# A hybrid encoder trunk on one core: the MLP up-projection turned from feature-major to token-major

## The chip, the cores and the metric

The kernel runs on one core of one Trainium2 chip. The metric is the device time of one execution in microseconds (us). A core has a matrix engine (TensorE, PE in the profile, with its weight loads as PEld), a vector engine (VectorE, DVE), a scalar engine (ScalarE, ACT), GpSimd (POOL) and SyncE (SP), which here only issues loads. Each engine works through its own queue of instructions in order; semaphores tie the queues together. TensorE writes to PSUM, eight banks of 128 partitions by 512 float32; everything else lives in SBUF, 128 partitions wide.

## The reference, cut to what matters

Two layers act on 256 tokens of 2048 features. Each layer is a token mixer followed by a gated MLP with a width-3 convolution over the positions:

```python
def conv_ffn(h, w_up, conv_w, conv_b, w_down):     # h: [1, 256, 2048], w_up: [2048, 2*5632]
    u = h @ w_up
    u = lax.conv_general_dilated(u, conv_w[:, None, :], window_strides=(1,), padding=((1, 1),),
                                 dimension_numbers=('NWC', 'WIO', 'NWC'),
                                 feature_group_count=u.shape[-1]) + conv_b
    gate, val = jnp.split(u, 2, axis=-1)
    return (jax.nn.silu(gate) * val) @ w_down

for i in range(2):
    h = h + mixer(rms_norm(h, mix_norm[i]))         # grouped-query attention, then dilated windows
    h = h + conv_ffn(rms_norm(h, ffn_norm[i]), w_up[i], conv_w[i], conv_b[i], w_down[i])
return rms_norm(h, final_norm)
```

All is float32. The up-projection makes 11264 columns, 5632 of the gate and 5632 of the value: 22 blocks of 512 columns in each layer, which the kernel takes as 11 pairs of a gate block and a value block.

## The kernel before, in words

**Precision.** TensorE works on a rounded float32 format. To keep accuracy each operand is split into a rounded high part and a low part that holds the rest (xh and xl for activations, wh and wl for weights), and a product is three products: xh wh, xl wh and xh wl.

**Weights.** A weight tile, called a raw, is 128 partitions by 1024 elements, 512 KB. SyncE loads raws into six buffers. ScalarE rounds a raw to wh (line 119) and VectorE subtracts to get wl (line 120), in `split_raw`. The pairs of wh and wl stand in a ring of three (`NHL = 3`); a split can begin when TensorE has finished with the pair three tiles earlier. The program order puts a split `AHEAD = 45` instructions earlier than where it is written. During the down-projection a fourth pair (tag `wh9`, `wl9`, in the MLP's pool) joins the ring.

**Two ways to multiply.** The mixers' projections use `feed`, which is token-major: 128 tokens of activations are the stationary operand, 512 weight columns stream through, and the result has tokens on the partitions (lines 164 to 166; per raw 12 matmuls of 512 columns). The up-projection uses `feed_T`, which is feature-major: 128 weight columns are the stationary operand, and the activations stream, xh and xl side by side, 512 columns for wh (line 143) and 256 for wl (line 146). Per raw that is 8 matmuls of each. The result has features on the partitions and tokens along the free axis, which is what the convolution wants, since its taps are then one number per partition and its neighbours lie along the row.

**Order of the MLP.** `ffn` walks the pairs p in two halves of 6 and 5 (`HALVES`). For each pair and each half of 256 columns (hh) it feeds the gate, starts `up_post` for it, feeds the value and starts `up_post` for that. `up_post` is a generator; `step()`, called once per raw, advances the oldest pending one to its next yield, so that the work behind a block is spread among the matmuls of the next. In `up_post` ScalarE takes the xl half out of PSUM (446), VectorE adds the xh half (447) and multiplies by the tokens' rstd (449; the row of rstd was broadcast over partitions with a matmul by ones in `bcast_rstd`), ScalarE applies the centre tap and the bias (451), VectorE the two outer taps (456, 458), and ScalarE the silu for a gate (461). For a value GpSimd multiplies gate and value (466, or 474) and the result is split into high and low (289, 290). Tokens are kept in an even and an odd half, with a zero column between them, which is why taps read reversed halves.

**Seven products.** The down-projection `project_pair` takes some chunks of 512 features (`SKG`: the first and third pair of the first half, the first of the second) as seven block products in place of eight; `glu_forms` writes their operand sums. The other chunks are plain. `side` is a generator (`bias_lines`) that prepares mixer B's bias tables in spare steps of layer 0's MLP.

## Time and profile before

| | |
|---|---|
| median of three runs | 2300.83 us (2300.44 to 2301.5) |
| the profiled execution | 2300.93 us, span from first to last instruction 2299.2 us |
| TensorE busy | 2281.6 us, 99% |
| VectorE busy | 1732.5 us, 75% |
| ScalarE busy | 1248.6 us, 54% |
| GpSimd busy | 168.5 us, 7% |
| loads, share of the 16 DMA engines | 58.3% |
| granted TensorE clock | 0.999 |

How to read it: the profile takes one execution. A row of the groups names line, engine, operation, output and inputs, shapes and count; then busy time, mean duration in ns, and the idle time just before these instructions with what ended it. Overlapping instructions share busy time, so the spacing of matmuls is read from their starts. A row of a window has the stretch, its length, and for each engine the busy us with the number of instructions in brackets; the last three columns are the granted clock, the share of DMA and GB/s. A row of the chain or the timeline has the start, the duration, the engine and the line.

### The profile page before, as it was taken

What the parts mean: (1) busy time and instruction counts of PE and PEld (TensorE: products, weight loads), DVE (VectorE), ACT (ScalarE), POOL (GpSimd) and SP (SyncE); (2) the same over time, 40 slices, a digit from 0 to 9 for tenths busy, and PEclk for the clock granted to TensorE, in tenths of its full rate; (3) what the DMA queues carried; (4) which work ended last, traced back from release to release, by engine and by line L of the source; (5) the groups of instructions that cost most, each with busy time, mean ns of one, the idle gap of its engine ahead of it and who ended that gap; (6) DMA issues with size and microseconds to landing.
All of it is one profiled execution on the core that took longest, in us unless ns stands there. A gap on an engine that the chain in (4) does not pass through costs nothing.

```text
span 2299.2 us, 31196 instructions
## 1 busy us (share of the span) xinstructions
PE 2281.6 (99%) x11581; PEld 1935.0 (84%) x11581; DVE 1732.5 (75%) x2483; ACT 1248.6 (54%) x1802; POOL 168.5 (7%) x130
## 2 busy tenths in 40 slices
PE   9999999999999999999999999999999999999998
PEld 7788788888888888888888888878888888888886
DVE  6877887777877778878876876576777788777774
ACT  6565565555545556445454454445555555565553
POOL 2210000010001010010000000000101000001110
PEclk9999999999999999999999999999999999999999
DMA  8444565765666555666655555566565566565663
GB/s 300 154 141 156 189 197 175 245 202 186 207 196 191 186 184 181 207 215 202 190 176 178 178 188 168 176 190 192 189 192 187 173 217 202 184 191 185 202 211 128
DMA packets 260313, 437.54 MB, mean 190 GB/s; under 512 B 13904, under 2 KB 196944, under 8 KB 260160
## 3 DMA queue, kind: packets, MB, share of 16 engines
q1 hardware_dynamic: 258080, 429.84, 58.3%
q0 software_dynamic: 1648, 5.15, 0.8%
q8 instruction: 90, 1.47, 0.3%
q14 instruction: 63, 0.52, 0.1%
q10 hardware_dynamic: 432, 0.56, 0.1%
HBM read 429.20 MB, written 6.29 MB: 189 GB/s over the span
## 4 chain that ended last, share of the span: by engine, by line
PE 93%; DVE 3%; DMA 1%; issue 1%; POOL 1%; ACT 0%; SPq 0%; POOLq 0%; DVEq 0%; ACTq 0%
PE acc L143 28%; PE acc L146 14%; PE acc L165 11%; PE acc L166 11%; PE acc L164 11%; PE acc L272 5%; PE acc L274 5%; PE acc L277 5%; DVE wl L120 1%; DVE tT L333 1%; PE ps L304 1%; DMA raw<-in_w_up_dram 1%; PE ps L308 1%; PE ps L307 1%; PE ps L306 0%
## 5 line engine op out<-in xcount | busy, mean ns | idle before, releaser
L119 ACT ACTIVATE wh<-raw 128x1024 fp32r<-128x1024 f32 x822 | 866.4, 1059 | 780.0 <-PE acc L166 276.5
L120 DVE TENSOR_TENSOR wl<-raw,wh 128x1024 fp32r<-128x1024 f32 x822 | 1007.7, 1231 | 369.5 <-ACT wh L119 356.8
L143 PE MATMUL acc<-xh,wh 128*128 128x512 f32 x2816 | 707.2, 393 | 0.8 <-ACT wh L119 0.8
L143 PEld LDWEIGHTS acc<-xh,wh 128*128 128x128 f32 x2816 | 507.0, 189 | 93.2 <-ACT wh L119 1.6
L146 PEld LDWEIGHTS acc<-xh,wl 128*128 128x128 f32 x2816 | 384.1, 190 | 27.5
L146 PE MATMUL acc<-xh,wl 128*128 128x256 f32 x2816 | 392.6, 282 | 0.0
L165 PE MATMUL acc<-wl,xh 128*128 128x512 f32 x768 | 300.2, 391 | 3.5 <-DVE wl L120 2.1
L164 PE MATMUL acc<-wh,xh 128*128 128x512 f32 x768 | 301.8, 394 | 0.0
L166 PE MATMUL acc<-wh,xh 128*128 128x512 f32 x768 | 299.5, 390 | 0.0
L272 PE MATMUL acc<-wh,ah 128*128 128x512 f32 x524 | 205.7, 393 | 0.0
L274 PE MATMUL acc<-wh,al 128*128 128x512 f32 x524 | 205.2, 392 | 0.0
L165 PE MATMUL acc<-wl,ah 128*128 128x512 f32 x480 | 188.0, 392 | 2.0 <-DVE wl L120 1.8
L164 PE MATMUL acc<-wh,ah 128*128 128x512 f32 x480 | 187.8, 391 | 0.0
L166 PE MATMUL acc<-wh,al 128*128 128x512 f32 x480 | 187.3, 390 | 0.0
L165 PEld LDWEIGHTS acc<-wl,xh 128*128 128x128 f32 x768 | 144.4, 188 | 34.0 <-DVE wl L120 4.6
L166 PEld LDWEIGHTS acc<-wh,xh 128*128 128x128 f32 x768 | 144.2, 188 | 30.0
L164 PEld LDWEIGHTS acc<-wh,xh 128*128 128x128 f32 x768 | 144.4, 188 | 27.8
L277 PE MATMUL acc<-wl,ah 128*128 128x512 f32 x524 | 146.9, 391 | 0.0
L466 POOL TENSOR_TENSOR cv<-cg,cv 128x512 f32<-128x512 f32 x32 | 73.2, 2288 | 651.6 <-DVE cv L458 591.2
L272 PEld LDWEIGHTS acc<-wh,ah 128*128 128x128 f32 x524 | 98.4, 188 | 22.0 <-ACT wh L119 0.2
L277 PEld LDWEIGHTS acc<-wl,ah 128*128 128x128 f32 x524 | 98.4, 188 | 21.8
L274 PEld LDWEIGHTS acc<-wh,al 128*128 128x128 f32 x524 | 98.4, 188 | 21.6
(175 smaller groups left out, 1838.9 us busy)
## 6 DMA issues: line engine op xcount, KB each, us to landing
raw<-in_w_up_dram SPq DMA_DIRECT2D x352, 512.0 KB, 5.0
raw<-in_w_down_dram SPq DMA_DIRECT2D x176, 512.0 KB, 4.4
raw<-in_w_b_dram SPq DMA_DIRECT2D x144, 512.0 KB, 4.2
raw<-in_w_bo_dram SPq DMA_DIRECT2D x48, 512.0 KB, 3.7
raw<-in_w_a_dram SPq DMA_DIRECT2D x40, 512.0 KB, 3.7
raw<-in_w_ao_dram SPq DMA_DIRECT2D x32, 512.0 KB, 3.6
raw<-in_w_a_dram SPq DMA_DIRECT2D x16, 256.0 KB, 6.5
h<-in_x_dram SPq DMA_DIRECT2D x4, 512.0 KB
```

The source lines that it names most:

```text
L119: nc.scalar.activation(wh, r, AF.Copy)
L120: nc.vector.tensor_tensor(wl, r, wh.bitcast(F32), ALU.subtract)
L143: nc.tensor.matmul(acc[j], wh[:, kt, j * P:(j + 1) * P], lhs[4 * kg + kt][2], start=first and i == 0 and kt == 0, stop=False)
L146: nc.tensor.matmul(acc[j][:, :NT], wl[:, kt, j * P:(j + 1) * P], lhs[4 * kg + kt][0], start=False, stop=end and kt == 3)
L164: nc.tensor.matmul(accs[m], xh, wh[:, j, :], start=st, stop=False)
L165: nc.tensor.matmul(accs[m], xh, wl[:, j, :], start=False, stop=False)
L166: nc.tensor.matmul(accs[m], xl, wh[:, j, :], start=False, stop=sp)
L272: nc.tensor.matmul(acc[k], xh, wh[:, j, :], start=k in fresh, stop=False)
L274: nc.tensor.matmul(acc[k], xl, wh[:, j, :], start=False, stop=False)
L277: nc.tensor.matmul(acc[k], xh, wl[:, j, :], start=False, stop=last[k] == i and j == 1)
L304: nc.tensor.matmul(o, lh[ls], rh[rs], start=start, stop=stop)
L466: nc.gpsimd.tensor_tensor(cv, cg, cv, ALU.mult)
```

## The change

The up-projection goes through `feed`, token-major, like the mixers' projections. `feed_T` and `bcast_rstd` are gone. A block is now 512 columns at once, so a pair makes one gate block and one value block. The result has tokens on the partitions, and `up_post` turns it:

- ScalarE takes each of the two accumulators (128 tokens by 512 features) out of PSUM, scaled by the token's rstd, which is now one number per partition (line 420 of the changed kernel).
- VectorE transposes each 32x32 block in its place (421), for 128x512 at once.
- Sixteen copies of 32 partitions by 256 elements (4 groups of 128 features, 2 halves of tokens, 32 tokens) bring the 32x32 blocks to their partitions. A string, `PLACE`, gives each to an engine: nine to GpSimd (432), seven to ScalarE (434), none to VectorE.
- The taps, the silu and the product follow as before, in two halves (441, 445, 447, 450, 455 or 463).

Buffers: u has two of 1032 columns in place of three of 516; s and t, the scaled and the turned block, have one each; cg and cv have three each in place of two. The first pair of each layer uses `project2`, which does three quarters of K for gate and value first. A second pool `wp` is opened around the MLP's pool and takes the taps, six operand tags and the fourth buffer pair.

```diff
+PLACE = "pappaappapappapa"
...
-    def feed_T(acc, lhs, w, n, hh, kgs, first, last):
...
     def ffn(l, hT, ss_in, g_next, last, side=None):
-        with tc.tile_pool(name=nm("fpool"), bufs=1) as fp:
+        with tc.tile_pool(name=nm("wpool"), bufs=1) as wp, tc.tile_pool(name=nm("fpool"), bufs=1) as fp:
+            cw = wp.tile([P, 448], F32, name=nm("cw"))[:, :NROW]
...
-            us = [fp.tile([P, 528], F32, name=nm("u"))[:, :516].rearrange("p (j c) -> p j c", j=2) for _ in range(3)]
+            us = [fp.tile([P, 1040], F32, name=nm("u"))[:, :1032].rearrange("p (j c) -> p j c", j=4) for _ in range(2)]
...
-            def up_post(acc, n, hh, c, after=None):
+            def up_post(acc, n, cs, after=None):
                 u = us.pop(0)
                 us.append(u)
...
+                s = fp.tile([P, 2, 512], F32, tag="s", name=nm("s"))
+                t = fp.tile([P, 2, 512], F32, tag="t", name=nm("t"))
+                for m in range(2):
+                    nc.scalar.activation(s[:, m], acc[m], AF.Copy, scale=rstd[:, m:m + 1])
+                    nc.vector.transpose(t[:, m], s[:, m])
+                yield
+                tv = t.rearrange("p m (j q c) -> p j m q c", j=4, q=4)
+                uv = u.rearrange("p j (m t) -> p j m t", m=2)
+                for i in range(16):
+                    if i == 8:
+                        yield
+                    a, b = i // 4, (i // 4 + i) % 4
+                    dst = uv[32 * b:32 * b + 32, :, :, 32 * a:32 * a + 32]
+                    src = tv[32 * a:32 * a + 32, :, :, b]
+                    if PLACE[i] == "p":
+                        nc.gpsimd.tensor_copy(dst, src)
+                    elif PLACE[i] == "a":
+                        nc.scalar.activation(dst, src, AF.Copy)
+                    else:
+                        nc.vector.tensor_copy(dst, src)
+                for hh in range(2):
+                    yield
+                    c = cs[hh]
+                    for j in range(2):
+                        nc.scalar.activation(halves(c[:, j]), halves(u[:, 2 * hh + j])[:, :, :P], AF.Identity,
+                                             bias=tap(n, 2 * hh + j, 3), scale=tap(n, 2 * hh + j, 1))
...
+                    if p == 0:
+                        va = project2(w_up[l], p, NPAIR + p, hT, kgs, 1,
+                                      lambda a, cg=cg: start(up_post(a, 0, cg)))
+                    else:
+                        start(up_post(project(w_up[l], p, hT, kgs), p, cg))
+                        va = project(w_up[l], NPAIR + p, hT, kgs)
+                    start(up_post(va, NPAIR + p, cv, after))
...
-                hl_ring.insert(0, (fp, 9))
+                hl_ring.insert(0, (wp, 9))
```

What stands in a row on ScalarE while it finishes a value block of layer 0's first half (wh is the split of a coming tile, ah the high part of the gated product, v the copy out of PSUM, u and cv the convolution's input and output; in brackets, the queues whose semaphores it waits for). Before:

```order
L446 ACTIVATE v_4488<-acc_4234 128x256 [waits PE_49]
L446 ACTIVATE v_4488<-acc_4235 128x256 [waits PE_49]
L119 ACTIVATE wh_4549<-raw_4523 128x1024 [waits DMAHW6_49,DVE_49,PE_49]
L451 ACTIVATE cv_4231<-u_2603,cw_2602 128x256 [waits DVE_49]
L451 ACTIVATE cv_4231<-u_2603,cw_2602 128x256
L119 ACTIVATE wh_4573<-raw_4569 128x1024 [waits DMAHW3_49,PE_49,Activation_49]
L289 ACTIVATE ah_3994<-cv_4231 128x256 [waits Pool_49]
L289 ACTIVATE ah_3996<-cv_4231 128x256 [waits DVE_49]
```

And now, from the second evacuation on (s is the scaled block, t the turned one):

```order
L420 ACTIVATE s_4638<-acc_4416,rstd_2597 128x512
L120 ACTIVATE wh_4696<-raw_4669 128x1024 [waits DMAHW6_49,DVE_49,PE_49]
L434 ACTIVATE u_2607<-t_4639 32x8x32 [waits DVE_49]
L434 ACTIVATE u_2607<-t_4639 32x8x32 [waits Pool_49]
L434 ACTIVATE u_2607<-t_4639 32x8x32 [waits Activation_49] x2
L434 ACTIVATE u_2607<-t_4639 32x8x32 [waits Pool_49]
L434 ACTIVATE u_2607<-t_4639 32x8x32 [waits Activation_49]
L120 ACTIVATE wh_4723<-raw_4719 128x1024 [waits DMAHW7_49,PE_49]
L434 ACTIVATE u_2607<-t_4639 32x8x32 [waits Activation_49]
L441 ACTIVATE cv_4216<-u_2607,cw_2594 128x256 [waits Activation_49,Pool_49]
L441 ACTIVATE cv_4216<-u_2607,cw_2594 128x256
L441 ACTIVATE cv_4217<-u_2607,cw_2594 128x256
```

Seven placements and a tap that waits for GpSimd now stand between the splits, where two taps stood that waited for VectorE.

GpSimd's queue held one product for each half of a value block, and nothing between them. The first five of layer 0, before:

```order
L474 TENSOR_TENSOR cv_2628<-cg_2627,cv_2628 128x512 [waits DVE_49,Activation_49,Pool_49]
L474 TENSOR_TENSOR cv_2848<-cg_2847,cv_2848 128x512 [waits DVE_49,Activation_49]
L466 TENSOR_TENSOR cv_3075<-cg_3074,cv_3075 128x512 [waits DVE_49,Activation_49,Pool_49]
L466 TENSOR_TENSOR cv_3299<-cg_3298,cv_3299 128x512 [waits DVE_49,Activation_49,Pool_49]
L474 TENSOR_TENSOR cv_3525<-cg_3524,cv_3525 128x512 [waits DVE_49,Activation_49,Pool_49]
```

Now, for one value block, the two products behind its nine copies, and the next gate block's copies after them:

```order
L432 COPY u_2607<-t_4241 32x8x32 [waits DVE_49]
L432 COPY u_2607<-t_4241 32x8x32 x2
L432 COPY u_2607<-t_4241 32x8x32 [waits Pool_49] x4
L432 COPY u_2607<-t_4241 32x8x32 [waits Activation_49]
L432 COPY u_2607<-t_4241 32x8x32 [waits Pool_49]
L455 TENSOR_TENSOR cv_3804<-cg_3802,cv_3804 128x512 [waits DVE_49,Pool_49]
L455 TENSOR_TENSOR cv_3805<-cg_3803,cv_3805 128x512 [waits DVE_49]
L432 COPY u_2606<-t_4438 32x8x32 [waits DVE_49]
```

The first copy waits for VectorE's second turn of the block, several wait for an earlier copy into the same partitions, and one for a placement of ScalarE there.

112 lines of the change are left out of this document (29 added, 83 removed).

## The prediction

> **What bounds the kernel now.** I read the page first, for its busy shares and the chain that ended last, then the groups of instructions by line, then two windows and the chain in order of time. The page:
>
> ```profile
> span 2299.2 us, 31196 instructions
> ...
> PE   2281.6 (99%) x11581; PEld 1935.0 (84%) x11581; DVE 1732.5 (75%) x2483; ACT 1248.6 (54%) x1802; POOL 168.5 (7%) x130
> ...
> PE 93%; DVE 3%; DMA 1%; issue 1%; POOL 1%; ACT 0%; SPq 0%; POOLq 0%; DVEq 0%; ACTq 0%
> ```
>
> TensorE is busy for 99% of the span and carries 93% of the chain. So a change is worth what it does to the spacing of matmuls, less whatever it makes TensorE wait. The waits of the up-projection in the groups, with the prices that I need from them:
>
> ```profile
> L119 ACT ACTIVATE wh<-raw 128x1024 fp32r<-128x1024 f32 x822 | 866.4, 1059 | 780.0 <-PE acc L166 276.5 <-PE acc L143 209.9 <-PE acc L274 122.7
> L120 DVE TENSOR_TENSOR wl<-raw,wh 128x1024 fp32r<-128x1024 f32 x822 | 1007.7, 1231 | 369.5 <-ACT wh L119 356.8
> L143 PE MATMUL acc<-xh,wh 128*128 128x512 f32 x2816 | 707.2, 393 | 0.8 <-ACT wh L119 0.8
> L146 PE MATMUL acc<-xh,wl 128*128 128x256 f32 x2816 | 392.6, 282 | 0.0
> ```
>
> The matmuls of the up-projection waited 0.8 us in all. ScalarE's split L119 waited 209.9 us for TensorE to give a buffer pair back: the splits run ahead and are held by the ring of three pairs. The busy times of L143 and L146 overlap, so the spacing comes from the chain (one tile of weights, 512 KB, is 8 matmuls of L143 and 8 of L146), and for the token-major form, which the projections of the mixers use already, from a window of mixer B in which nothing else stands on TensorE:
>
> ```profile
> 673.18 1.84 PE acc L143 x8
> ...
> 843.57 1.84 PE acc L143 x8
> ```
> ```profile
> 1074.00:1109.00 35.00, 35.00 (x156) 1.00 0.68 211
> 700.00:880.00 180.00, 180.00 (x1035) 158.50 (x1034) 135.37 (x201) 105.63 (x158) 18.80 (x9) 1.00 0.60 188
> ```
>
> Between the two chain rows lie 61 tiles: 170.39 / 61 = 2.793 us each. The first window has about 155 starts of 512 columns in 35 us, or 0.2265; with the edges I take 0.227, and 12 of them, one tile token-major, are 2.725 us. In the second window, all up-projection, VectorE is busy for 75% and ScalarE for 59%.
>
> **The change part by part.**
>
> (1) Matmuls. The up-projection has 22 blocks of 512 columns in each of 2 layers, 8 tiles each: 352 tiles before and after. 352 x (2.793 - 2.725) = 23.9 us less, all on the path. Two matmuls of `ones` with the diagonal of rstd go too, under 1 us in all; I leave them out.
>
> (2) Work taken off and put on, per block of 512 columns, from these rows:
>
> ```profile
> L447 DVE TENSOR_TENSOR v<-acc,v 128x256 f32<-128x256 f32 x176 | 65.9, 416 | 0.0
> L449 DVE TENSOR_TENSOR u<-v,rbc 128x512 f32<-128x512 f32 x88 | 60.9, 692 | 2.8
> L446 ACT ACTIVATE v<-acc 128x256 f32<-128x256 f32 x176 | 56.4, 371 | 0.0
> L451 ACT ACTIVATE cv<-u,cw 128x256 f32<-128x256 f32 x88 | 48.2, 595 | 13.0 <-DVE u L449 13.0
> L458 DVE SCALAR_TENSOR_TENSOR cv<-u,cw,cv 128x256 f32<-128x256 f32 x88 | 38.5, 478 | 0.0
> L289 ACT ACTIVATE ah<-cv 128x256 fp32r<-128x256 f32 x84 | 30.7, 410 | 105.3 <-POOL cv L466 75.3 <-POOL cv L474 30.0
> L290 DVE TENSOR_TENSOR al<-cv,ah 128x256 fp32r<-128x256 f32 x84 | 32.6, 421 | 52.4 <-ACT ah L289 52.2
> L333 DVE STREAM_TRANSPOSE tT<-h 32x256 f32<-32x256 f32 x144 | 62.8, 436 | 2.6
> L677 ACT ACTIVATE stg<-acc,rstd 128x512 f32<-128x512 f32 x34 | 23.0, 680 | 9.8 <-PE acc L166 9.4
> ```
>
> VectorE loses 4 adds (L447) and 2 multiplications (L449): 3.05 us. It gains 2 turns of 128x512: L333 is 0.436 for 256 elements, and 256 more cost 0.27 (L449 against L447), so 0.70 each, 1.4 us. ScalarE loses 4 copies of L446 (1.5 us) and gains 2 scaled evacuations at 0.68 (L677) and 7 placements, priced as the plain copy L289, 0.41: 4.2 us. Against a tile time of 2.725 x 8 = 21.8 us per block: ScalarE 8 splits at 1.06 (8.5), 4.2, four L451 (2.4), half a silu and a share of L289 (1.4) make 16.5; VectorE 8 splits at 1.23 (9.8), 1.4, eight L456/L458 (3.8), L290 (0.8) make 15.9. Neither is full.
>
> (3) GpSimd gets 9 copies of 32 partitions x 256 elements per block. No such copy is in the trace. The rows on both sides of it:
>
> ```profile
> L797 POOL TENSOR_TENSOR t<-stg,st_q 128x256 f32<-128x256 f32 x16 | 17.1, 1100 | 80.7 <-ACT stg L677 80.7
> L729 POOL TENSOR_TENSOR ct_k<-rp,gb 128x128 f32<-128x128 f32 x2 | 0.9, 455 | 22.0 <-DMA gb<-in_k_gain_dram 22.0
> L49 POOL MEMSET ones<- 128x128 f32 x1 | 0.2, 205 | 0.0
> L431 POOL MEMSET u<- 128x2 f32 x6 | 0.4, 122 | 0.0
> ```
> ```profile
> 106.67 0.73 POOL L797 TENSOR_TENSOR t<-stg,st_q 128x256 f32<-128x256 f32 x1 [20.21 <-ACT stg L677]
> ```
>
> Above: a product with two inputs of the same 8 x 32 pattern, 0.73 undisturbed. Below: a fill that reads nothing; 128x2 to 128x128 adds 0.083, so 256 elements are 0.29. A copy reads one stream. The product adds 0.73 - 0.455 = 0.276 per 128 elements, 2.2 ns each, over a start of 0.18; half of that slope for one stream gives 0.18 + 0.28 = 0.46. I take 0.45 and keep 0.29 and 0.73 for the range.
>
> The mean of L797 is 1.10, not 0.73, and that matters more than the copy itself:
>
> ```profile
> 527.25 3.46 DVE L120 TENSOR_TENSOR wl<-raw,wh 128x1024 fp32r<-128x1024 f32 x2
> ```
> ```profile
> 527.39 2.24 POOL L466 TENSOR_TENSOR cv<-cg,cv 128x512 f32<-128x512 f32 x1 [20.11 <-DVE cv L458]
> ```
>
> The first subtraction ends at 527.25 + 1.23 = 528.48; GpSimd's product, issued at 527.39, ends at 529.63, 1.15 later; the second subtraction ends at 530.71, 1.08 after that. Each waited for the other to finish. The Trainium skill (SBUF — State Buffer, Who interferes with whom) says this as a rule: a VectorE instruction with two SBUF inputs and a GpSimd instruction that reads SBUF exclude each other for a whole instruction. By that rule, the trace agrees, with 1.15 and 1.08. So each copy is 0.3 us (0.45 less what runs before the lock) of VectorE's time where a subtraction is due, and one of the copies can sit behind a subtraction for 1.08.
>
> (4) The wait that is added. On ScalarE the convolution's centre tap (L441 after) needs all 16 placements, and behind it stand the next splits. How long may that last? A pair comes free when TensorE leaves it and is wanted two tiles on, 5.45 us later; the split takes 1.06 + 1.23. That leaves some 3 us.
>
> A value block, with 0 where TensorE ends it. ScalarE: the split of tile 2 to 1.25, the second evacuation to 1.85; VectorE: its subtraction to 2.5, the second turn to 3.15. GpSimd's nine copies from 3.15: 9 x 0.42 = 3.8, and behind the subtractions of tiles 3 and 4 twice 1.08, so 9.0. Three centre taps, 0.5 apart, then the split of tile 5 to 11.6. VectorE: five L445/L447 from 9.65, 0.4 apart as 0.478 with overlap, to 11.8; then the product of gate and value holds the lock for 1.15, to 13.0; the subtraction of tile 5 to 14.1. TensorE reaches tile 5 at 13.63 and needs its low half one matmul later, 13.85: it waits 0.25. For 22 value blocks, 5 us.
>
> A gate block has no product: four taps end at 11.2, the split of tile 5 at 12.2, the subtraction at 13.45. It makes it by 0.4. No loss, and nothing in hand.
>
> Three pairs in each layer write the seven operand sums: in the second half of such a block VectorE has eight operations of L290's kind where a plain one has two, 6 x 0.34 (0.42 with overlap) = 2.0 us, around the next block's first tiles, where the same count leaves a plain block about 1 us. I put 1 us on each: 6 us.
>
> (5) Free edits. The loads stay 352 of 512 KB, in longer runs; TensorE waited for none of them. If that cover went, a tile could come late by what the issue queue lost, which no row prices. The projection's last quarter of K in the first pair is needed 12 tiles in, 32.7 us, before 6 tiles in; it can only be less late. The fourth buffer pair is in another pool; only the down-projection uses it, and its matmuls wait as before. The u-gap fill is 2 instructions in place of 3.
>
> Sum: 2300.9 of the profiled execution (span 2299.2, the rest around it; the median of the runs is 2300.83, the same) - 23.9 + 5 + 6 = 2288.
>
> **The rivals.**
>
> A, the forecast: GpSimd's copy between 0.41 and 0.50. The loss per value block is 0 to 0.6, and the seven-sum blocks cost 3 to 6 us: 2280 to 2296. Chance 0.36.
>
> B, everything hidden: the copy at 0.40 or less. The last copy then starts before the subtraction of tile 4 asks for the lock, the taps begin at 3.15 + 9 x 0.38 + 1.08 = 7.7, and tile 5 is ready 0.65 early. Only the seven-sum blocks cost anything: 2277 to 2283. For it: a fill's 0.29. Against: no reading instruction on GpSimd is that fast here. Chance 0.25. The Trainium skill (GPSIMD Engine Reference, 4.1 Engine selection) says that one-input work on GpSimd runs at roughly line rate; by it the copy would be about 0.4 us, an estimate from that page's 1.2 GHz, and the sum 2280; no run here shows it.
>
> C, slower: GpSimd's chain of copies becomes what the taps wait for. At 0.73 the nine copies are 2.5 us longer; value blocks then lose 2.75 and gate blocks 2.1: 22 x 4.85 = 107, so 2300.9 - 23.9 + 107 = 2384. It decides from the copy price at which 44 blocks lose 24 us, 0.51. For it: the mean 1.10 of L797 beside VectorE's work. Against: half the input. Chance 0.19, for 2306 and above. The Trainium skill (Perfetto Trace Analysis, Optimizing Scalar/DVE Operations) warns that moving work between VectorE and GpSimd may not help because of the shared port; the rows above agree that there is a price, and C is where it wins.
>
> D, slower: ScalarE's placements cost what its patterned tap copy costs, 0.595 (L451), not 0.41: 7 x 0.19 = 1.3 us more ahead of the same split. Value blocks lose 1.0 more, gate blocks 0.8: 40 us, 2328. Against: L451 carries two per-partition operands, which the placement has not. Chance 0.10.
>
> E, no change: gain and waits cancel, copy at about 0.51: 2296 to 2306. Chance 0.10.
>
> **How the numbers follow.** Runs of this kernel spread by 1.1 us; 0.2%, 4.6 us, is about what can be told from no change. Faster is A and B, 0.61; same 0.10; slower C and D, 0.29. The likeliest is A, with its sum of 2288. The range goes from 2275, B with its full 24 us and a little, to 2330, which takes in D and the milder part of C and leaves out about 0.12 above. The faster cases alone are 2276 to 2296.
>
> **What would show it.** (1) Token-major chain rows 2.73 us per tile, and TensorE's busy share 98 to 99%. (2) GpSimd's copies: undisturbed 0.45, mean nearer 0.6. (3) In the releasers of the up-projection's matmuls, VectorE's low half (wl) with 5 to 15 us, most in value blocks at tile 5; if gate blocks wait as much, the copies are dearer than I took. (4) ScalarE's tap line waiting for GpSimd's copies, 1 to 2 us a block. (5) VectorE's subtraction with a mean of about 1.35. Wrong would be: GpSimd's copy over 0.5, a tap line waiting 4 us or more, or TensorE waiting for ScalarE's wh instead of wl.

## The result, and the profile after

The changed kernel takes 2330.5 us (four runs, 2327.7 to 2332.5) against 2300.9 beside it: a ratio of 1.0128, interval 1.0110 to 1.0145. It is slower, by 29.6 us, where 13 us faster were forecast. The page of the profiled execution, its busy shares and its chain:

```profile
span 2328.9 us, 28808 instructions
...
PE 2278.9 (98%) x10169; PEld 1859.0 (80%) x10169; DVE 1667.5 (72%) x2301; ACT 1366.7 (59%) x2022; POOL 388.4 (17%) x524
...
PE 72%; DVE 12%; POOL 7%; ACT 4%; issue 3%; DMA 3%; SPq 0%; DVEq 0%; POOLq 0%; ACTq 0%
```

TensorE has 1412 matmuls fewer, and its share of the chain fell from 93% to 72%: VectorE, GpSimd and ScalarE now stand on the chain for 23%. The groups that answer to those quoted before:

```profile
L121 DVE TENSOR_TENSOR wl<-raw,wh 128x1024 fp32r<-128x1024 f32 x822 | 1005.4, 1230 | 449.9 <-ACT wh L120 446.0
L432 POOL COPY u<-t 32x256 f32<-32x256 f32 x396 | 213.9, 540 | 827.7 <-DVE t L421 806.8
L434 ACT ACTIVATE u<-t 32x256 f32<-32x256 f32 x308 | 129.2, 420 | 52.3 <-POOL u L432 27.5 <-DVE t L421 18.4
L421 DVE STREAM_TRANSPOSE t<-s 128x512 f32<-128x512 f32 x88 | 62.1, 706 | 9.2 <-ACT s L420 9.2
L270 ACT ACTIVATE ah<-cv 128x256 fp32r<-128x256 f32 x84 | 30.7, 411 | 108.7 <-POOL cv L455 77.3 <-POOL cv L463 31.4
```

The prices are those of the forecast: the turn 0.706, the placement on ScalarE 0.420. GpSimd's copy has two durations: 338 of the 396 take under 0.45 us (median of all 0.40), the other 58 take 1.28 to 1.48, and the mean is 0.54. VectorE's subtraction keeps its mean, 1.230. What TensorE waited for (us in total, times, longest), after:

```profile
PE acc L146 <- DVE wl L121: 12.8, 20, 0.9
PE acc L258 <- DVE wl L121: 8.0, 11, 1.7
PE acc L253 <- ACT wh L120: 6.5, 7, 1.4
PE acc L145 <- ACT wh L120: 5.3, 3, 4.0
PE ps L393 <- DMA cr<-in_conv_dram: 2.0, 1, 2.0
```

L258 and L253 are the seven-product down-projection, whose matmuls waited for nothing before. The next table gives the eight MLP stages in us, read from the profiled execution, each from its first matmul to the first of the next stage (0a is layer 0's first half; `up` and `dn` are its projections; dn 0b and dn 1b are the seven-product part alone, up to the first plain matmul). Without a wait, token-major blocks need 21.8 us, so the up stages need 261.6 and 218.0. All that the table leaves out is within 0.4 us of each other in the first two rows; the last column is the median of the runs.

| kernel | up 0a | dn 0a | up 0b | dn 0b | up 1a | dn 1a | up 1b | dn 1b | median us |
|---|---|---|---|---|---|---|---|---|---|
| before | 274.5 | 126.6 | 223.4 | 53.6 | 269.8 | 126.9 | 223.5 | 53.7 | 2300.9 |
| changed | 285.4 | 132.6 | 221.6 | 58.2 | 272.3 | 132.1 | 221.8 | 57.8 | 2330.5 |
| GpSimd copies left out | 279.7 | 129.1 | 220.1 | 56.9 | 268.3 | 128.9 | 220.1 | 57.1 | 2309.0 |
| last blocks unplaced | 286.5 | 125.1 | 224.0 | 53.0 | 274.5 | 125.1 | 224.0 | 53.0 | 2313.7 |
| fourth pair in ring | 284.0 | 131.6 | 217.6 | 55.8 | 270.7 | 130.2 | 217.6 | 55.9 | 2315.1 |
| placements uncrossed | 284.6 | 129.4 | 222.4 | 57.0 | 272.1 | 128.6 | 222.6 | 58.2 | 2321.2 |
| product on VectorE | 280.0 | 127.7 | 217.9 | 55.4 | 266.2 | 127.4 | 217.8 | 56.6 | 2295.5 |
| same, idle product on GpSimd | 283.3 | 130.3 | 220.1 | 59.4 | 270.3 | 130.1 | 220.9 | 58.2 | 2319.5 |
| low half last | 281.8 | 133.0 | 218.4 | 59.4 | 268.5 | 132.1 | 218.4 | 59.7 | 2318.7 |
| best version | 268.2 | 125.1 | 217.6 | 53.0 | 262.5 | 125.1 | 217.6 | 53.0 | 2267.2 |

So the up-projections lost 9.8 us in sum and the down-projections 19.9, with nothing changed in the latter's own work. What happens at such a start, on ScalarE, GpSimd and TensorE in order of time (start, duration, engine, line; in brackets the idle time before and its releaser):

```profile
568.87 1.09 ACT L441 ACTIVATE cv<-u,cw 128x256 f32<-128x256 f32 x2 [1.56 <-POOL u L432]
569.87 1.04 ACT L120 ACTIVATE wh<-raw 128x1024 fp32r<-128x1024 f32 x1
...
582.56 0.72 ACT L270 ACTIVATE ah<-cv 128x256 fp32r<-128x256 f32 x2 [2.68 <-POOL cv L455]
583.19 1.04 ACT L120 ACTIVATE wh<-raw 128x1024 fp32r<-128x1024 f32 x1
```
```profile
561.15 7.69 POOL L432 COPY u<-t 32x256 f32<-32x256 f32 x9 [19.32 <-DVE t L421]
571.42 2.13 POOL L455 TENSOR_TENSOR cv<-cg,cv 128x512 f32<-128x512 f32 x1 [2.58 <-DVE cv L447]
579.18 3.35 POOL L455 TENSOR_TENSOR cv<-cg,cv 128x512 f32<-128x512 f32 x1 [5.63 <-DVE cv L447]
```
```profile
570.96 0.50 PE L253 MATMUL acc<-wh,ah 128*128 128x512 f32 x1 [0.54 <-ACT wh L120]
...
580.29 1.20 PE L258 MATMUL acc<-wl,ah 128*128 128x512 f32 x4 [0.88 <-DVE wl L121]
...
584.28 0.50 PE L253 MATMUL acc<-wh,ah 128*128 128x512 f32 x1 [1.41 <-ACT wh L120]
```

Twice ScalarE stands at an instruction that needs GpSimd: at the tap until the nine copies end (7.69 us in place of 9 x 0.40), and at ah until the product ends. The split of a coming tile (wh) is behind it in the queue, and TensorE waits for that split. I call this the queue-head theory. Its rivals: that GpSimd's work costs by holding up VectorE (port), or that the stretch simply holds too much work (supply).

### The profile page after: what moved, and what is told of

It reads as the page before. It is cut to its first block, busy times and chain, and to the rows that moved or that the text cites. A ratio compares the mean times of both kernels' runs of the same rounds, so it can differ in the third digit from the quotient of the medians.

```text
span 2328.9 us, 28808 instructions
## 1 busy us (share of the span) xinstructions
PE 2278.9 (98%) x10169; PEld 1859.0 (80%) x10169; DVE 1667.5 (72%) x2301; ACT 1366.7 (59%) x2022; POOL 388.4 (17%) x524
## 3 DMA queue, kind: packets, MB, share of 16 engines
q1 hardware_dynamic: 122912, 429.84, 56.6%
q8 instruction: 79, 1.29, 0.2%
## 4 chain that ended last, share of the span: by engine, by line
PE 72%; DVE 12%; POOL 7%; ACT 4%; issue 3%; DMA 3%; SPq 0%; DVEq 0%; POOLq 0%; ACTq 0%
PE acc L146 20%; PE acc L147 19%; PE acc L145 19%; DVE wl L121 5%; POOL u L432 4%; PE acc L258 4%; PE acc L253 3%; PE acc L255 3%; ACT wh L120 2%; POOL cv L455 2%; DVE tT L314 1%; DVE cv L445 1%; DVE cv L447 1%; POOL cv L463 1%; DMA raw<-in_w_up_dram 1%
## 5 line engine op out<-in xcount | busy, mean ns | idle before, releaser
L146 PE MATMUL acc<-wl,xh 128*128 128x512 f32 x2176 | 855.6, 393 | 13.5 <-DVE wl L121 11.1
L145 PE MATMUL acc<-wh,xh 128*128 128x512 f32 x2176 | 854.6, 393 | 5.9 <-ACT wh L120 5.3
L147 PE MATMUL acc<-wh,xh 128*128 128x512 f32 x2176 | 850.2, 391 | 0.0
L146 PEld LDWEIGHTS acc<-wl,xh 128*128 128x128 f32 x2176 | 409.8, 188 | 115.5 <-DVE wl L121 32.2
L145 PEld LDWEIGHTS acc<-wh,xh 128*128 128x128 f32 x2176 | 410.2, 189 | 93.0 <-ACT wh L120 8.4
L147 PEld LDWEIGHTS acc<-wh,xh 128*128 128x128 f32 x2176 | 409.7, 188 | 83.9
L432 POOL COPY u<-t 32x256 f32<-32x256 f32 x396 | 213.9, 540 | 827.7 <-DVE t L421 806.8
L253 PE MATMUL acc<-wh,ah 128*128 128x512 f32 x524 | 205.5, 392 | 6.7 <-ACT wh L120 6.5
L434 ACT ACTIVATE u<-t 32x256 f32<-32x256 f32 x308 | 129.2, 420 | 52.3 <-POOL u L432 27.5
L258 PE MATMUL acc<-wl,ah 128*128 128x512 f32 x524 | 148.4, 394 | 8.2 <-DVE wl L121 8.0
L258 PEld LDWEIGHTS acc<-wl,ah 128*128 128x128 f32 x524 | 96.7, 188 | 35.9 <-DVE wl L121 16.5
L253 PEld LDWEIGHTS acc<-wh,ah 128*128 128x128 f32 x524 | 98.3, 188 | 32.3 <-ACT wh L120 11.5
L255 PEld LDWEIGHTS acc<-wh,al 128*128 128x128 f32 x524 | 98.4, 188 | 20.3
L146 PEld LDWEIGHTS acc<-wl,ah 128*128 128x128 f32 x480 | 90.2, 188 | 23.9 <-DVE wl L121 5.7
L147 PEld LDWEIGHTS acc<-wh,al 128*128 128x128 f32 x480 | 90.1, 188 | 18.5
L145 PEld LDWEIGHTS acc<-wh,ah 128*128 128x128 f32 x480 | 90.2, 188 | 18.3
```

Source lines behind the costliest of these rows:

```text
L145: nc.tensor.matmul(accs[m], xh, wh[:, j, :], start=st, stop=False)
L146: nc.tensor.matmul(accs[m], xh, wl[:, j, :], start=False, stop=False)
L147: nc.tensor.matmul(accs[m], xl, wh[:, j, :], start=False, stop=sp)
L253: nc.tensor.matmul(acc[k], xh, wh[:, j, :], start=k in fresh, stop=False)
L255: nc.tensor.matmul(acc[k], xl, wh[:, j, :], start=False, stop=False)
L258: nc.tensor.matmul(acc[k], xh, wl[:, j, :], start=False, stop=last[k] == i and j == 1)
```

## The experiments

Ratios are to the kernel before, run beside each.

**The copies left out.**

```diff
-                nc.gpsimd.memset(u[:, :, P:P + 1], 0.0)
+                nc.gpsimd.memset(u, 0.0)
...
                     if PLACE[i] == "p":
-                        nc.gpsimd.tensor_copy(dst, src)
+                        continue
```

> The changed kernel with GpSimd's nine placement copies of every up-projection block left out (u is filled with zeros once instead, so nine sixteenths of each turned block never reach it and the values are not the reference's); ScalarE's seven placements, taps and products stay. Theory 'queue heads': splits come late because ScalarE and VectorE stand at instructions that wait for GpSimd, its copies and its products; without the copies the wait for them (1.56 us on ScalarE at 568.9 of the changed kernel's trace, followed by a TensorE gap of 0.9 us) is gone, the wait for the products stays: about 1.5 us in each of the four down-projection starts, 2 in each first pair and 0.1 in each plain value block, 2315 to 2322 us in all. Theory 'copies and port': the copies and what they do to VectorE are the loss, so about 25 us go, 2303 to 2308. Theory 'split supply': VectorE and ScalarE cannot deliver the short units' splits and sums fast enough whatever GpSimd does; down-projections stay at 132 and 58 us, 2326 to 2331.

2309.0 us, 1.0040 (1.0027 to 1.0054). Between the forecast of the queue heads (2315 to 2322) and that of copies and port (2303 to 2308): 21.5 us go, though the undisturbed copies are as cheap as 0.40. `Supply` falls.

**Splits placed earlier.**

```diff
-AHEAD = 45
+AHEAD = 70
```

> The changed kernel with AHEAD 70 in place of 45: the splits are placed further ahead of the side work in ScalarE's and VectorE's queues. Theory 'queue heads': some of the splits now stand before the instructions that wait for GpSimd; the down-projection starts lose 2 to 4 us less each and the first pairs 2 less: 2310 to 2322 us. Theories 'copies and port' and 'split supply': the same work in another order, within 4 us of 2330.

2324.9 us, 1.0104 (1.0089 to 1.0119): 5.6 us back, 2.6 and 2.1 of them in the long down-projections and at most 0.7 either way in any other stage. In the order of ScalarE, splits moved ahead of ah in the second half of the last block, not ahead of the taps. The time lies between the forecasts, 2.9 us above that of the queue heads and 1.1 below the others', so this run decides nothing.

**The fourth pair of buffers in the ring.**

```diff
                 slots, forms = {}, {}
+                if side is None and hf == 0:
+                    hl_ring.insert(0, (wp, 9))
...
-                hl_ring.remove((wp, 9))
+                if hf == 1:
+                    hl_ring.remove((wp, 9))
```

> The changed kernel with the fourth pair of split buffers in use in all of layer 1 and from the first down-projection of layer 0 on, where the changed kernel uses it in the down-projections alone. One more pair is 12 matmuls, 2.7 us, of work in hand. If the waits in the up-projection are bursts a little longer than the slack of three pairs, the up-projection stages that have the pair (3 of 4, which lose 3.6, 10.7 and 3.8 us against matmuls without a wait: 218.0, 261.6, 218.0) lose half of that or less, and the down-projection starts, whose ring is filled earlier, 2 us less each: 2312 to 2320 us. If VectorE and ScalarE lack time and not slack, the gain is under 4 us: 2326 to 2331. Layer 0's first up-projection half stays at 285 in both.

2315.1 us, 1.0058 (1.0043 to 1.0073), as the slack theory said. The second halves reach 217.6, no wait at all. Layer 1's first half gained only 1.6 and the stage ahead of it lost 4.3: the pair stood first in the ring and its first split came late there. I put that down to its buffer being shared with the stage before. This was not tried by itself; with the pair behind the others in the ring ("All of it together" below) the stage ahead loses nothing.

**The last value block of each half without turn and placements.**

```diff
-                    nc.vector.transpose(t[:, m], s[:, m])
+                    if n != short:
+                        nc.vector.transpose(t[:, m], s[:, m])
...
-                for i in range(16):
+                for i in range(0 if n == short else 16):
...
                 slots, forms = {}, {}
+                short = NPAIR + p1 - 1
```

> The changed kernel without VectorE's turn and without the sixteen placements in the last value block of each half (four blocks; their taps then read what the buffer held before, so the values are not the reference's). Theories 'queue heads' and 'copies and port': the down-projection starts lose their first part, the wait at 570 and before; 126 to 129 and 54 to 56 us in place of 132 and 58, 2314 to 2321 us in all; the wait for GpSimd's products (1.57 and 1.86 us) stays. Theory 'split supply': the turn's 1.4 us of VectorE alone are saved: at most 1.4 us in each of four, 2325 to 2330.

2313.7 us, 1.0056 (1.0039 to 1.0073). The down-projections fall to 125.1 and 53.0, below the kernel before and below the 126 to 129 and 54 to 56 forecast; `supply` (at most 1.4 us from each) falls here too. ScalarE still stands 98.3 us before ah in all, but TensorE has no wait at L253 or L258 any more. So the loss there comes from the turn and the placements of the last block, and the wait for the product alone does not make it. The up stages rose by 1.1 to 2.4, in their last two blocks; I take it that the shortened chain now meets the last tiles of the up-projection, which no run shows.

**Placements that do not cross.** Four placements write each row group of u; in the changed kernel both engines take turns at it, and each waits for the one before.

```diff
-PLACE = "pappaappapappapa"
+PLACE = "ppaapaapaappappa"
```

> The changed kernel with the placements shared out by the row group of u that they write: GpSimd has all eight that write rows 0 to 63, ScalarE all eight that write rows 64 to 127, so that none of the two engines' placements waits for one of the other's. In the changed kernel four placements of one row group are written in turn by both engines, each waiting for the one before. Theory 'crossed placements' (the 27.5 us for which ScalarE stood before its placements waiting for GpSimd's, with splits queued behind, are what leaving the copies out gave back): most of those 21.5 us come back without leaving anything out, 2311 to 2318 us. Theory 'copies and port' (the copies' own time and what they do to VectorE): one copy in nine fewer gives a ninth of it, 2326 to 2330.

2321.2 us, 1.0088 (1.0073 to 1.0103). Between the two forecasts. GpSimd has eight copies here in place of nine. ScalarE no longer waits at L434 for a copy (27.5 us before), though it waits 14.2 in place of 7.0 at the taps, and 9.4 us come back, 7.5 of them in the down-projections. That is less than half of what the copies cost. How the rest of their 21.5 us parts into their own time and their collisions with VectorE is not shown.

**The product's split one step later.**

```diff
                 nc.gpsimd.tensor_tensor(cv, cg, cv, ALU.mult)
                 yield
+                yield
```

The same line is added in `glu_forms`.

> The changed kernel with the splits of the gated product (ah, al) written one step later than the product on GpSimd, two steps of side work behind it and not one. Theory 'queue heads': ScalarE stood 77.3 and 31.4 us before ah, waiting for GpSimd's products, with splits behind it; one step later it stands less: each down-projection start loses 1.5 to 2 us less, each first pair 1 to 3 less, 2316 to 2323 us. If those waits were idle time that cost nothing: 2327 to 2333.

2325.5 us, 1.0106 (1.0091 to 1.0121). A miss: ScalarE's wait for the product grew (82.0 and 35.5 us for 77.3 and 31.4) and the first pairs kept their loss. The first up stage fell by 7.8, since the fetch gap of the next run did not occur there, and layer 0's first down-projection rose to 136.5. This rise is the same gap, moved by the extra step: SyncE issued eight stores at 539 to 550, and a fetch behind them came late. VectorE stood for it, and TensorE 5.3 us at 553.9:

```profile
539.24 3.07 SPq L888 DMA_DIRECT2D scr<-lnt  x4
544.55 5.07 SPq L888 DMA_DIRECT2D scr<-lnt  x4
```
```profile
551.45 1.23 DVE L222 TENSOR_TENSOR raw<-raw,raw 128x1024 f32<-128x1024 f32 x1 [6.92 <-DMA raw<-in_w_down_dram]
```

So only layer 1 shows what the edit does to a down-projection: 129.6 for 132.1 in its first half, 58.6 for 57.8 in its second.

**Two late transfers in layer 0.**

```diff
             def taps_gen():
-                yield
+                for _ in range(3):
+                    yield
...
-                    nc.sync.dma_start(dst[:, 32 * i:32 * i + 32, :], ln[:, :w])
+                    nc.gpsimd.dma_start(dst[:, 32 * i:32 * i + 32, :], ln[:, :w])
```

> The changed kernel with two edits in layer 0's first up-projection half, at places 150 us apart: the transposes of the taps come two steps later (TensorE waited 2.2 us for their rows at 278.7 and ran at half speed for a while behind it), and the stores of the bias lines go through GpSimd's queue, not through the one that fetches weights (a gap of 4.2 us at 433 behind eight stores that took 2.4 us each while fetches queued behind them). Theory 'late transfers': both gaps and the slow matmuls behind them go, the stage falls from 285.4 to 274 to 277 us and the whole to 2319 to 2322. If the fetches are late for another reason, the first gap alone goes: 281 to 282 and 2326 to 2327. Nothing else changes, the later stages within 0.5 us each.

2323.0 us, 1.0098 (1.0081 to 1.0115); the stage falls from 285.4 to 278.5, both about 1 us above the forecast. Both gaps are gone: the first block loses 1.5 in place of 5.1, and the block of the gap 0.4 in place of 7.4. Three later blocks lose 3.8 more together, beside the stores that GpSimd now issues. SyncE's queue held these stores beside the loads, eight of them from 406.8 to 423.8 with two fetches between them. With the stores on GpSimd's queue the gap occurs in none of the runs, and in the run of the later split, where eight fetches followed the first four stores, it did not occur at this place. The stores ahead of the weight fetches had thus made the 4 us gap.

**All of it together.** The last three edits, the fourth pair (behind the others in the ring), and ordinary units ahead of the first short one:

```diff
+                if hf == 0:
+                    first = "ccc" + "Pc" * 4 + "P" + "Pc" * 4 + "P" + "Pc" * 4 + "c"
+                else:
+                    first = "cccc" + "Pc" * 7 + "ccccc"
```

> The last three edits together, with the fourth pair of split buffers in the ring from layer 0's first down-projection on and in all of layer 1 (there behind the other three, since put first it waited for the stage before, 4.2 us), and with three or four ordinary units ahead of the first short product unit in the first down-projection pair of each half. If the losses are separate bursts, each with its own wait, the gains add up until nothing is left to lose: up-projections of 275 to 277, 218, 263 to 266 and 218 us, down-projections of 126 to 128 and 53 to 55, 2275 to 2290 us in all, faster than the kernel before. If they share one cause (VectorE and ScalarE too full), the sum stops near the best single edit: 2305 to 2312.

2303.8 us, 1.0012 (1.0003 to 1.0022). Between the two forecasts (2275 to 2290, and 2305 to 2312), close to the second. The up stages came as forecast (276.6, 217.6, 264.9, 217.6), the down-projections did not (134.5, 57.2, 129.1, 57.3). One wait had grown. ScalarE and GpSimd of this kernel at layer 1's start (ah is L270, the product L456):

```profile
1849.62 3.89 ACT L120 ACTIVATE wh<-raw 128x1024 fp32r<-128x1024 f32 x4
1860.69 0.42 ACT L270 ACTIVATE ah<-cv 128x256 fp32r<-128x256 f32 x1 [7.18 <-POOL cv L456]
```
```profile
1857.40 3.26 POOL L456 TENSOR_TENSOR cv<-cg,cv 128x512 f32<-128x512 f32 x1 [9.39 <-DVE cv L448]
```

The four splits ahead of ah use up the ring; then ScalarE stands 7.2 us, because the product began late, behind VectorE's taps and sums, and took 3.3 us.

**The product on VectorE.** This is the single edit with the largest gain; it is made in `glu` and in `glu_forms`.

```diff
-                nc.gpsimd.tensor_tensor(cv, cg, cv, ALU.mult)
+                nc.vector.tensor_tensor(cv, cg, cv, ALU.mult)
```

> The changed kernel with the gated products (44 of 128x512) on VectorE in place of GpSimd, nothing else. Theory 'queue heads': the product takes VectorE about 0.75 us (its 128x512 instructions with two inputs, estimated from the 0.42 us of the 128x256 ones) where GpSimd took 2.4 to 4.4 us and began after another engine's wait; ScalarE's wait before ah (77.3 and 31.4 us) shrinks to a third, and the down-projection starts lose 2 to 4 us less each, the first pairs 1 to 3 less: 2312 to 2322 us. Theory 'VectorE too full': 33 us more of work on the engine that is the tightest beside TensorE costs more than it gives: 2330 to 2340.

2295.5 us, 0.9978 (0.9969 to 0.9987): 35 us less than the changed kernel, 5 below the kernel before, and far below both forecasts (the lower was 2312 to 2322). The wait and the product in its groups:

```profile
L270 ACT ACTIVATE ah<-cv 128x256 fp32r<-128x256 f32 x84 | 31.0, 409 | 41.6 <-DVE cv L455 32.5 <-DVE cv L463 9.1
L455 DVE TENSOR_TENSOR cv<-cg,cv 128x512 f32<-128x512 f32 x32 | 21.9, 685 | 0.4
```

The product takes 0.685 us here and took 2.43 on GpSimd (L455 of the changed kernel); the wait before ah falls from 108.7 to 41.6 us. The ordinary value blocks, which lost 0.4 each, lose nothing, and the first pairs' largest loss falls from 5.0 to 2.3.

**The same edit in the kernel before,** as a control.

> A control: the kernel before, with its 44 gated products on VectorE in place of GpSimd and nothing else. In its trace ScalarE stood as long before ah, waiting for GpSimd's products (75.3 and 30.0 us), as in the changed kernel (77.3 and 31.4), yet TensorE has hardly a gap above 0.25 us in its up-projections and down-projection starts. If the wait costs only where the turned chain has used up the slack (theory 'queue heads' as an interaction), nothing is there to gain: 2297 to 2303 us. If the product on GpSimd costs as much in any kernel, the 35 us of the changed kernel would show here too: 2265 to 2280. If VectorE, with 33 us more of work, is too full in the kernel before: 2303 to 2315.

2300.3 us, 0.9999 (0.9989 to 1.0009): nothing to gain, as an interaction demands. The wait before ah in the kernel before, and in this one:

```profile
ACT ah L289 <- POOL cv L466: 75.3, 32, 3.1
```
```profile
L289 ACT ACTIVATE ah<-cv 128x256 fp32r<-128x256 f32 x84 | 30.6, 403 | 8.8 <-DVE cv L466 7.3 <-DVE cv L474 1.5
```

Some 96 of the 105 us of ScalarE's waiting went, and nothing was gained. So the wait costs only together with the change; the next figures show that the change used up much of what covered it.

**Where the cover went.** For each tile I took the time from the end of its low half's subtraction to its first matmul with that half. In us, median of a stage:

| kernel | up 0a | up 0b | up 1a | up 1b |
|---|---|---|---|---|
| before | 5.8 | 5.8 | 5.8 | 5.8 |
| before, low half first | 3.3 | 3.4 | 3.3 | 3.4 |
| changed | 2.1 | 2.2 | 1.8 | 1.8 |
| changed, low half last | 3.2 | 3.5 | 3.3 | 3.5 |
| product on VectorE | 2.6 | 3.0 | 2.4 | 2.8 |
| best version | 3.8 | 7.3 | 6.5 | 7.3 |

The changed kernel has a third of the cover, and 43 of its 352 tiles have less than 0.1 us; with the product on VectorE these are 10. Part of it is the order of matmuls in a unit. Feature-major, all eight with the high half came first; token-major, the second matmul wants the low half. Two runs change that order alone, one way in each kernel; in the first the edit is in `feed`, which the mixers use too:

```diff
                 nc.tensor.matmul(accs[m], xh, wh[:, j, :], start=st, stop=False)
-                nc.tensor.matmul(accs[m], xh, wl[:, j, :], start=False, stop=False)
-                nc.tensor.matmul(accs[m], xl, wh[:, j, :], start=False, stop=sp)
+                nc.tensor.matmul(accs[m], xl, wh[:, j, :], start=False, stop=False)
+            for m, kt in order:
+                (wh, wl), j = hls[kt // 2], kt % 2
+                xh, xl = at(lhs[4 * kg + kt], m)
+                nc.tensor.matmul(accs[m], xh, wl[:, j, :], start=False, stop=last and kt == 3)
```

> The changed kernel with the matmuls of a token-major unit in another order: first the four (or eight) pairs that use the high half wh, then those that use the low half wl; nothing else. wl is then used after 8 matmuls and not after 1, 1.6 us later. Theory 'order takes the slack': the 48 waits over 0.15 us between the first and the second matmul of a unit in the up-projections, 23.1 us in all and none over 1.6 us, are covered, less what comes back because VectorE is not let catch up: the up-projections lose 12 to 20 us less in all, the down-projection starts as before (they have this order already), 2308 to 2318 us. Theory 'total work in the way' (the queues are late whatever the order): the waits move to the next unit's wh, under 5 us gained, 2325 to 2331.

2318.7 us, 1.0078 (1.0063 to 1.0093). The up stages gain 14.0 us (3.6, 3.2, 3.8, 3.4), inside the 12 to 20 forecast; the down-projections lose 3.5 more. Outside the table, layer 0's first mixer takes 4.8 us less (264.7 for 269.5), which was not forecast, the next 0.8 less and the end 2.4 more. The whole is just above its range, and would be further above without the mixer. In the kernel before:

```diff
             for kt, j in order:
                 nc.tensor.matmul(acc[j], wh[:, kt, j * P:(j + 1) * P], lhs[4 * kg + kt][2],
                                  start=first and i == 0 and kt == 0, stop=False)
-            for kt, j in sorted(order, key=lambda o: o[1]) if end else order:
                 nc.tensor.matmul(acc[j][:, :NT], wl[:, kt, j * P:(j + 1) * P], lhs[4 * kg + kt][0],
                                  start=False, stop=end and kt == 3)
```

> The kernel before with the feature-major units in the opposite order: each matmul with the low half right behind the one with the high half, where all eight with the high half stood first. If the order alone made the difference, 10 us or more are lost, 2310 to 2325. If the order takes 1.6 us of a slack of 5.8 us and the rest is the longer chain of the turned blocks, hardly a wait appears: 2300 to 2304 us.

2305.6 us, 1.0022 (1.0012 to 1.0032), 1.6 above the upper range. The cover falls to 3.4 us and still TensorE waits 0.8 us for the low half in all its up-projection; the 5 us come without waits, as 2.7 us in each second half. The order is worth 2.4 us of cover in this kernel and 1.1 to 1.7 in the changed one, out of about 4 that went. I put the rest down to the turned block's chain; no run parts it.

**Port or queue head?** GpSimd repeats the product into a scratch tile that nobody reads, behind VectorE's own.

```diff
+                nc.vector.tensor_tensor(cv, cg, cv, ALU.mult)
-                nc.gpsimd.tensor_tensor(cv, cg, cv, ALU.mult)
+                nc.gpsimd.tensor_tensor(junk().rearrange("p (j t) -> p j t", j=2), cg, cv, ALU.mult)
```

> The kernel with the products on VectorE (2295.5 us), and beside it GpSimd multiplies the same 44 pairs of 128x512 again into a scratch tile that nobody reads, right behind VectorE's product. GpSimd works and reads as much as in the changed kernel, and its next placement copies still stand behind the product, but nobody waits for the product. Theory 'queue heads': ScalarE's wait for the product was the cost; 2295 to 2302 us. Theory 'port': GpSimd's product beside VectorE's two-input instructions was the cost; 2322 to 2332.

2319.5 us, 1.0077 (1.0060 to 1.0094): neither forecast. 24 of the 35 us that moving the product had gained are lost again. The ordinary value blocks stay at no loss, as queue heads said. The first pairs lose as much as in the changed kernel (5.4 and 4.4 in the first halves, 2.3 in the second) and the down-projections nearly as much (378.0 us in all for 380.7, and 367.1 without the idle product), although nobody waits for this product. VectorE's small instructions beside it, in this kernel, in the changed one, and in the one with the product on VectorE, from which this run differs by the idle product alone:

```profile
L271 DVE TENSOR_TENSOR al<-cv,ah 128x256 fp32r<-128x256 f32 x84 | 45.5, 573 | 0.0
L445 DVE SCALAR_TENSOR_TENSOR cv<-u,cw,cv 128x256 f32<-128x256 f32 x88 | 57.0, 666 | 5.6 <-ACT cv L441 5.6
```
```profile
L271 DVE TENSOR_TENSOR al<-cv,ah 128x256 fp32r<-128x256 f32 x84 | 32.6, 421 | 54.1 <-ACT ah L270 54.0
L445 DVE SCALAR_TENSOR_TENSOR cv<-u,cw,cv 128x256 f32<-128x256 f32 x88 | 44.9, 524 | 5.7 <-ACT cv L441 5.6
```
```profile
L271 DVE TENSOR_TENSOR al<-cv,ah 128x256 fp32r<-128x256 f32 x84 | 32.3, 417 | 0.0
L445 DVE SCALAR_TENSOR_TENSOR cv<-u,cw,cv 128x256 f32<-128x256 f32 x88 | 40.1, 475 | 3.8 <-ACT cv L441 3.7
```

The idle product starts a little later than the real one and falls on al and the next taps: these take 0.15 us longer in the mean than in the changed kernel, 25 us over both rows, and 0.16 and 0.19 longer than without the idle product. So GpSimd's product costs VectorE time though nobody waits for it. The next copies stand behind it in GpSimd's queue as well, and ScalarE's wait for them at L434 rises from 21.9 to 28.6 us. How the loss in the changed kernel's first pairs and down-projection starts parts between port and queue head is not settled, since the idle product collides with other instructions than the real one did.

**A version that beats both.** The edits of "All of it together", with the product on VectorE in place of the later step:

> The kernel of the last run of all edits together, with the products on VectorE in place of one step later. There one wait was left in each down-projection start: ScalarE stood 7.2 us at ah for a product that GpSimd began late and took 3.3 to 4.4 us for, with the next splits behind it, and TensorE waited 2.1 to 3.4 us and then ran slowly for 3.4 us. Theory 'queue heads': that wait falls below what four pairs of buffers cover, the down-projections come to 126 to 128 and 53 to 55 us, and the whole to 2284 to 2292 us, faster than the kernel before. Theory 'VectorE too full': 2300 to 2310.

2271.5 us, 0.9872 (0.9857 to 0.9887), below the forecast. The same without the reordered units:

> The same without the ordinary units put ahead of the short ones in the down-projections. If the short product units at the start, with their sums and splits on VectorE beside the last value block's chain, take part in the loss, the four down-projection starts lose 1 to 3 us more each: 4 to 10 us above the run with them. If the wait for GpSimd alone made it, within 2 us of that run.

2275.2 us, 0.9889 (0.9872 to 0.9905): 3.8 us of loss, 3.1 of it in the down-projections and just under the 4 to 10 forecast, so the short units at the start take a small part. And with the low half last:

> The best version so far (2271.5 us) with the same order of matmuls in its token-major units. Its up-projections of layer 0's first half lose 6.6 us against 261.6 and layer 1's 0.9; 'order takes the slack' gives 3 to 6 us: 2265 to 2269. 'Total work in the way': 2270 to 2273.

2267.2 us, 0.9855 (0.9840 to 0.9869), 33.7 us less than before. The time is in the forecast range, but not for its reason: all eight stages are as in the 2271.5 us version, to 0.1 us, and the 4.3 us come from layer 0's first mixer, 4.7 us shorter, which uses the same `feed`. The engines' shares of its chain, and what TensorE still waited for in these projections:

```profile
PE 86%; DVE 0%; issue 0%; ACT 0%; POOL 0%; POOLq 0%; DVEq 0%
```
```profile
PE acc L145 <- ACT wh L120: 0.9, 2, 0.7
PE acc L150 <- DVE wl L121: 0.6, 1, 0.6
```

Three of its four up stages lose under 1 us and all four down-projections none; the 6.6 us left are in layer 0's first half. The up stages take 965.9 us in all, 25.3 less than before: where little waits, the token-major form is worth what step (1) said. Of the rest, 4.6 us are in the down-projections and 3.5 in the mixers and at the end. The edits that a feature-major kernel can have too (the fourth pair, the late transfers, the order of units) were not tried on the kernel before, so the 33.7 us are not the form's alone.

## Why the prediction was wrong

The sum against the trace: before, the up stages took 991.2 us in all; 352 tiles at 2.725 are 959.2. The changed kernel's took 1001.0, a loss of 41.8, and the down-projections 19.9 more than before: 2300.9 - 32.0 + 41.8 + 19.9 = 2330.6.

(1) Matmuls: right, 21.8 us per block wherever nothing waits. The gain was 32.0, not 23.9, since the stages before were 8.1 us longer than 352 tiles at 2.793.

(2) Work on VectorE and ScalarE: right in each price (0.706, 0.420, 0.676 for the scaled evacuation). "Neither is full" held in the mean and decided nothing.

(3) GpSimd's copy: 0.40 undisturbed, below the 0.45 taken. That is rival B's condition, for which 2277 to 2283 was forecast, so the copy's price was not what decided. The collision was read rightly (58 copies of 1.28 to 1.48 us), but it did not lengthen the subtractions: mean 1.230, where 1.35 was to show.

(4) The added wait: right for ordinary value blocks (0.3 to 0.4 us for the 0.25 forecast) and gate blocks (0 to 0.2). The three pairs at 1 us failed: the block in which the first pair's value is finished lost 5.0 in the first halves and 1.4 in the second, with 1.2 and 0.5 before it, 16.2 in all against 4 for those four. I counted VectorE's extra operations and left out what GpSimd's product does there: with it on VectorE, 5.0 becomes 2.3 and 1.4 becomes 0.2. ScalarE's stand at ah for that product was in the row of L289 before, with 105.3 us, and had cost nothing there; whether the stand or VectorE's slower instructions beside the product cost more here is open. The wait that the step did price, the tap's for the copies, was 7.0 us in six times (L441), not 1 to 2 us a block; ScalarE stood for copies at its placements instead, 27.5 us in 42 times (L434).

(5) "The fourth buffer pair is in another pool; only the down-projection uses it, and its matmuls wait as before" is the step that failed worst: its matmuls, which had waited for nothing, waited 8.0 us at L258 and 6.5 at L253, and the down-projections took 19.9 us more where nothing was added. What the step left out is the last value block, whose work falls into the start of the down-projection: it is twice as large as before, with the turn and the placements added to its chain. Without these two the down-projections took 356.2 us, against 360.8 before and 380.7 with them. The unpriced "a tile could come late" cost about 7 us once, where eight stores of the bias lines stood ahead of weight fetches, and the taps' rows, 2.0 us late at 278.6, 3.8 with the slow matmuls behind.

The slack of "some 3 us" in step (4) is right only for tiles that nothing delays: their low half is ready about 3.1 us ahead. The median was 1.8 to 2.2 us where the kernel before had 5.8. Of the rivals none was the mechanism: C had the sign, through an undisturbed price of copies above 0.51, which was not reached, and D's 2328 lies near the result by luck, since its price (0.595) was 0.420. The range ended at 2330, 0.5 us short.

## What to carry to other kernels

When the form of a matmul changes, look at how long before its use each operand is ready, and not only at the engines' load: taking the product from GpSimd took away most of 105 us of ScalarE's waiting and gained nothing with 5.8 us of cover; with about 2 us of cover it gained 35. An instruction that waits for another engine's result holds up all that is queued behind it, so follow the longest chain through the engines at the places where two stages overlap, and move its slowest step to the engine that is already there. Work that hands a tile over in turns between two engines is better divided so that they never meet.

## What the runs showed of the hardware that was not expected

After a wait of about 2 us TensorE can run at half speed for a while. Layer 0's taps made it wait 2.0 us, and a little later each matmul of 512 columns takes 0.427 us from start to start in place of 0.227, eight of them, 3.4 us:

```profile
280.97 0.30 PE L393 MATMUL ps<-ident,cr 96*128 96x96 f32 x1 [2.01 <-DMA cr<-in_conv_dram]
...
282.54 0.63 PE L147 MATMUL acc<-wh,xh 128*128 128x512 f32 x1
282.97 0.63 PE L145 MATMUL acc<-wh,xh 128*128 128x512 f32 x1
```
```profile
437.00:441.00 4.00, 2.97 (x6) 2.08 (x7) 3.46 (x8) 2.98 (x7) 0.00 (x0) 0.50 0.44 138
```

The second row is the stretch behind the 4 us fetch gap: a granted clock of 0.50. The Trainium skill (TensorE: Matmul & The Clock Gate, Part 1: The HAM clock gate) says that the clock falls to half after an idle window of about 3.4 us; here 2.0 us of waiting was enough, so the measurement differs. A wait of 2 us thus cost up to 1.6 us (8 x 0.200) more than itself. It need not: with the low half last, a wait of 2.27 us at 1656 was followed by matmuls at full speed (granted clock 1.00 from 1656 to 1660). In the run with the idle product, a wait of 1.89 us at 930 was followed by a granted clock of 0.66 to 935, and one of 1.90 at 2225 by 1.00. What decides between the two is not shown.

A product of 128x512 in float32 took 0.685 us on VectorE and 2.43 on GpSimd. The Trainium skill (GPSIMD Engine Reference, 4.1 Engine selection) calls GpSimd about half as fast for two inputs; beside VectorE's own two-input work it was 3.5 times slower here. Of the 44 products on GpSimd one took 1.29 us and the others 2.13 to 3.35.
